# mLSTM gate rows during the retention gate tiles, one scan for samples and prompt, and unread products ahead of TensorE's first operands

## The chip, the cores and the metric

The kernel runs on one core of a Trainium2 chip. The metric is the device time of one execution in microseconds; three executions of the kernel before took 1385.29, 1387.02 and 1387.32 us, median 1387.02. A profiled execution of the same kernel is the source of every row shown. Engines are named as in the profile: PE (TensorE), DVE (VectorE), ACT (ScalarE), POOL (GpSimd), SP (which issues most DMAs here). Each engine works through its own list of instructions in order.

## What is computed

One decoder layer for a prompt of 1024 tokens and for 8 samples of 8 tokens each (1088 token columns in all), width 1024. A combined projection feeds four retention heads and four mLSTM heads of 128; their outputs go through an output projection and a ConvFFN. The part that matters here:

```python
h = rmsnorm(x, pre_mix_g)
proj = (h @ w_in).astype(f32)
q_r, k_r, v_r, g_r, q_m, k_m, v_m, o_m = ...
gates = take(2 * N_ML_HEADS) + b_g.astype(f32)
i_pre, f_pre = gates[..., :N_ML_HEADS], gates[..., N_ML_HEADS:]
...
ret_y = head_groupnorm(ret_out, ret_g) * jax.nn.silu(g_r)
...
logf = jax.nn.log_sigmoid(fg)
def step(carry, inp):
    C, n, m = carry
    qc, kc, vc, ic, lfc = inp
    b = jnp.cumsum(lfc, axis=-1)
    logw = b[..., :, None] - b[..., None, :] + ic[..., None, :]
    logw = jnp.where(causal, logw, -jnp.inf)
    m_t = jnp.maximum(b + m[..., None], jnp.max(logw, axis=-1))
    ...
```

The stabiliser m_t follows the recurrence m_t = max(logf_t + m_(t-1), i_t). For the prompt it starts at -1e30, for each sample at that sample's own m0.

## The kernel before

The kernel is written against a tile framework that derives semaphores from the data and schedules each engine's list from its own time estimates; `issue_after` adds an ordering edge. So the order of the source and the order of an engine's list are not the same.

Tokens are taken in four blocks of 272 columns. A `dense` product (L156 to L160) of one 128-row output tile and one block is 24 matmuls of 128x272: eight slices of the contraction, for each of three terms (high part of the weight by high part of x, low by high, high by low). `proj` loads a weight tile (SP), splits it (high part on ACT, L144; low part on DVE, L146), and runs the four blocks into banks of a pool of two, `psA`; each block is evacuated by a function of its own, and a block's product cannot start before the block two earlier has been read out of its bank.

Opening: pieces of x and the first two weight tiles come in by DMA. For every block, `gain_split` writes the high part of x times a gain (`hh`, ACT, L198) and the low part (`hl`, DVE, L199), and `square_sum` squares x on ACT in two halves (L203) and adds up on DVE for the RMS norm. TensorE starts with the value products of retention heads 0 and 1 (weight tiles `in8` and `in9`), of block 0 in the order of `terms`, evacuated by ACT (`v_r`, L438). `in8_2` is the third block of tile `in8`.

Then follow q and k of retention head 0 (`evac_rot`, ACT L451 and L452, DVE L453 to L455, with rotation and norm), and the gate tiles of the four retention heads, `in12` to `in15`: `early_gate` makes z from the bank on DVE (L469), sigmoid on ACT (L470) and their product y on DVE (L471) for each of 16 tile blocks. Then `gate_proj` projects all mLSTM gates (L316), reads them out (ACT L319, DVE L320 to L322) and adds biases (ACT L323, L324) into two tiles of 4 partitions by 1088: `fg` and `ig`. During it the attention of retention head 0 runs.

`gate_rows` is a generator that turns these rows into what the mLSTM heads need: log sigmoid of the forget gate (ACT L345, L346, L352, L354; DVE L348 to L360), the cumulated sum b per chunk (DVE scan, L368), the stabiliser m by one scan over the prompt (L374) and eight scans of 8 columns over the samples (L378), then differences, exponentials and column copies (L381 to L414). A piece of it is issued at each `next(rows)`, which stands inside the heads that follow. All the while POOL sums up-projection weights in pieces of DRAM and SBUF traffic (`weight_sums`, L715).

Of the kernel before, what the change touches and what calls it, by code (L numbers as in the profile page):

```python
# [16 lines left out]
P = 128  # L17
# [75 lines left out]
def hybrid_layer_kernel(ctx: ExitStack, tc: tile.TileContext, a: dict, o: dict):  # L93
# [4 lines left out]
    def log_exp_tables(after=None):  # L98

        with tc.issue_after(after.ins) if after else nullcontext():  # L100
            nc.scalar.preload_act_table_set("natural_log_exp_and_others")

# [48 lines left out]

    def dense(ps, w, x, b, term=None):

        hi, lo = w
        for k in range(KT):
            ws = slice(k * P, (k + 1) * P)  # L156
            xh, xl = (t[:, k % 4, qcols(b)] for t in x[b // 2][k // 4])
            for i, (u, v) in enumerate(((hi, xh), (lo, xh), (hi, xl))):
                if term in (None, i):
                    nc.tensor.matmul(ps, u[:, ws], v, start=k == i == 0, stop=k == KT - 1 and i == 2)  # L160

    def rstd_small(out, v, w, name, shape):

        l = w.tile(shape, F32, tag="rs_l", name=f"l_{name}")
        nc.scalar.activation(l, v, AF.Ln)
# [27 lines left out]
    def gain_split(x, gain, ops, b):  # L193

        for k in range(KT):
            g = vec[:, gain + k:gain + k + 1]
            hi, lo = (t[:, k % 4, qcols(b)] for t in ops[k // 4])
            nc.scalar.activation(hi, x[:, k, :], AF.Copy, scale=g)  # L198
            nc.vector.scalar_tensor_tensor(lo, x[:, k, :], g, hi.bitcast(F32), ALU.mult, ALU.subtract)  # L199

    def square_sum(x, acc, sq, end=nc.vector):
        for i in range(2):
            nc.scalar.activation(sq[i], x[:, 4 * i:4 * i + 4, :], AF.Square)  # L203
        s, t = sq
# [22 lines left out]
    def tok(name, rows=P, dt=F32):  # L227
        return tokp.tile([P, T], dt, tag="tok", name=name)[:rows, :]


# [26 lines left out]
    sqs = [tok(f"sq{i}").rearrange("p (k n) -> p k n", k=4) for i in range(2)]  # L257
    for b in range(4):
        n = BLK[b][1]
        if b % 2 == 0:  # L260
            h.append(quadrants("h", b // 2))
        gain_split(xs[b], V_PREMIX, h[b // 2], b)
        nts.append(sums[b // 3][:, b % 3 * Q:(b % 3 + 1) * Q])
# [30 lines left out]
    def gate_proj():  # L294
        xst = m2.tile([P, X_SEL], F32, tag="vx", bufs=1, name="xst")
        nc.sync.dma_start(xst, a["cx"][:, :X_SEL])
        xsel = m2.tile([P, X_N - X_SEL], F32, tag="sb", bufs=1, name="xsel")
        nc.sync.dma_start(xsel, a["cx"][:, X_SEL:])
        nc.vector.tensor_copy(idb, ident)
        nc.vector.tensor_copy(negb, xst[:, X_NEG:X_NEG + P])  # L300
        for t in vts:
            nc.gpsimd.memset(t[:, :, P:P + 1], 1.0)
        nc.vector.tensor_copy(negsb, xst[:, X_NEGS:X_NEGS + TS])
        nc.scalar.activation(sel, xsel[:100, :].rearrange("p (j h c) -> p j h c", j=2, h=NH), AF.Copy)
        fg = tok("fg", NH)
        ig = yT[3][:NH, 0, :]
# [17 lines left out]
        nc.scalar.activation(ig, ig, AF.Identity, bias=vec[0:NH, V_BG + 1:V_BG + 2])  # L324

    uihl = mp.tile([100, T], F32R, name="uihl")
    cols = mp.tile([P, 9, 3 * NH], F32, name="cols")
# [12 lines left out]
    def gate_rows():  # L340
        fg, ig = gates
        stk = yT[2][:68, 0, :]
        nc.gpsimd.memset(stk, 0.0)
        e = stk[0:NH, :]
        nc.scalar.activation(e, fg, AF.Abs)  # L345
        nc.scalar.activation(e, e, AF.Exp, scale=-1.0)  # L346
# [6 lines left out]
        rw = yT[3][:NH, 1, :]  # L353
        nc.scalar.activation(rw, w1, AF.Exp, scale=-1.0)  # L354
        nc.vector.tensor_tensor(e, e, rw, ALU.mult)
# [12 lines left out]
        nc.vector.tensor_tensor_scan(bb, rst, lf, 0.0, ALU.mult, ALU.add)  # L368
# [5 lines left out]
        nc.vector.tensor_tensor_scan(mm[:, :LP], lf[:, :LP], ig[:, :LP], NEG, ALU.add, ALU.max)  # L374
        yield
        for s in range(NB):
            sl = slice(LP + s * LS, LP + (s + 1) * LS)
            nc.vector.tensor_tensor_scan(mm[:, sl], lf[:, sl], ig[:, sl], mst[:, 8 + s:9 + s], ALU.add, ALU.max)  # L378
        nc.scalar.activation(stk[0:NH, :], mm, AF.Exp, scale=-1.0)
# [3 lines left out]
        yield  # L383
        nc.sync.dma_start(o["m"], mend)
        u = mm
        nc.vector.tensor_tensor(u, bb, mm, ALU.subtract)
        yield
        aa = bb
        nc.vector.tensor_tensor(aa, ig, bb, ALU.subtract)
        yield  # L390
# [8 lines left out]
        nc.scalar.activation(stk[32:32 + NH, :], aa, AF.Exp)  # L399
        nc.scalar.activation(u, u, AF.Exp)  # L400
        put_rows(1, u)
# [62 lines left out]
    def early_gate(hid):  # L464
        def f(b, ps):
# [3 lines left out]
            nc.vector.tensor_tensor(z, ps, rb[:, o0:o0 + n], ALU.mult)  # L469
            last["sigmoid"] = nc.scalar.activation(y, z, AF.Sigmoid)  # L470
            nc.vector.tensor_tensor(y, y, z, ALU.mult)  # L471
# [19 lines left out]
    def mix_head(hd, ml):  # L491
# [15 lines left out]
        else:  # L507
# [236 lines left out]
    wsums = weight_sums()  # L744
    rows = iter(())
# [620 lines left out]
```

## Time and profile before

| what | us |
|---|---|
| median of three executions | 1387.02 |
| the profiled execution | 1385.24 |
| its span (first to last instruction) | 1383.5 |
| ACT busy | 594.7 |
| POOL busy | 452.4 |

The profiled execution is 1.74 us longer than its span. "Waits" rows read: engine and line that waited, the instruction waited for, then the sum, the count and the longest. Chain rows give start, length and what ran, following back from the last instruction of a window to what released it. Timeline rows give start, length, engine, line, operation, output and inputs, and in brackets the idle time before it with what ended it. A window's row gives the busy time and granted clock of that stretch.

The stages in time, by the profile: first products from 4.78 us, q and k of head 0 behind the values of heads 0 and 1, gate tiles to about 116 us, gates and the attention of head 0 to about 133 us, then retention heads 1 to 3 with the row work.

### The profile page before, as it was taken

How to read it: one execution, taken by the hardware profiler on the slowest of the kernel's cores; microseconds unless marked ns; L12 is line 12 of the kernel's file. 1: busy time of each engine (PE TensorE's matmuls, PEld its weight loads, DVE VectorE, ACT ScalarE, POOL GpSimd, SP SyncE). 2: the span in 40 equal slices, each digit the busy share in tenths (PEclk: the TensorE clock that was granted, in tenths of full speed). 3: DMA queues.
4: the chain of work that ended last, by engine and by line, in shares of the span. 5: the costliest groups of instructions: out<-in, count | busy, mean ns of one | idle time of the engine just before them, and what ended most of it. 6: DMA issues, size and time to landing. Idle time of an engine off the chain costs nothing.

```text
span 1383.5 us, 26841 instructions
## 1 busy us (share of the span) xinstructions
PE 1346.4 (97%) x10545; PEld 1320.3 (95%) x10545; DVE 1010.9 (73%) x2013; ACT 594.7 (43%) x1107; POOL 452.4 (33%) x572
## 2 busy tenths in 40 slices
PE   7999899999999999899999999999999999999995
PEld 7999889999999999899999999999999999999995
DVE  7747986475474366477899988787787788996677
ACT  7524543312322235445465434344344355554563
POOL 1544540379676000000453322222222206872000
PEclk9999999999999999999999999999999999999998
DMA  6444342376986210433214444434444459533363
GB/s 240 138 138 145 119 138 64 110 215 214 199 170 202 62 49 31 159 97 94 98 58 161 148 149 140 131 118 129 151 135 134 132 162 318 185 110 91 97 213 129
DMA packets 93166, 192.80 MB, mean 139 GB/s; under 512 B 16240, under 2 KB 41456, under 8 KB 92528
## 3 DMA queue, kind: packets, MB, share of 16 engines
q1 hardware_dynamic: 80736, 149.03, 33.1%
q0 software_dynamic: 12160, 41.95, 10.7%
q8 instruction: 83, 1.36, 0.4%
q14 instruction: 43, 0.35, 0.1%
q10 hardware_dynamic: 144, 0.11, 0.0%
HBM read 134.58 MB, written 56.47 MB: 138 GB/s over the span
## 4 chain that ended last, share of the span: by engine, by line
PE 88%; DVE 6%; ACT 3%; DMA 1%; issue 1%; SPq 0%; DVEq 0%; ACTq 0%
PE in L160 26%; PE up_S L994 6%; PE up_S L993 6%; PE up_S L992 6%; PE out L160 5%; PE dn L1191 5%; PE dn L1189 5%; PE dn L1190 5%; PE up_A L993 4%; PE up_A L992 4%; PE up_A L994 4%; ACT hh L198 1%; PE up_A L1037 1%; PE up_A L1038 1%; PE up_A L1036 1%
## 5 line engine op out<-in xcount | busy, mean ns | idle before, releaser
L160 PE MATMUL in<-hh,wh_in 128*128 128x272 f32 x1024 | 302.7, 298 | 12.5 <-ACT hh L198 7.9
L160 PE MATMUL in<-hl,wh_in 128*128 128x272 f32 x1024 | 297.0, 293 | 0.0
L160 PE MATMUL in<-hh,wl_in 128*128 128x272 f32 x1024 | 296.9, 292 | 0.0
L160 PEld LDWEIGHTS in<-hh,wh_in 128*128 128x128 f32 x1024 | 194.2, 190 | 17.9 <-ACT hh L198 8.5
L160 PEld LDWEIGHTS in<-hh,wl_in 128*128 128x128 f32 x1024 | 193.8, 190 | 3.6 <-issue 3.5
L160 PEld LDWEIGHTS in<-hl,wh_in 128*128 128x128 f32 x1024 | 193.3, 190 | 1.0 <-issue 0.9
L144 ACT ACTIVATE wh_up<-st_up 128x1024 fp32r<-128x1024 f32 x84 | 80.5, 959 | 162.2 <-PE up_S L993 99.2
L146 DVE TENSOR_TENSOR wl_up<-st_up,wh_up 128x1024 fp32r<-128x1024 f32 x84 | 95.7, 1139 | 9.1 <-ACT wh_up L144 9.1
L966 DVE TENSOR_TENSOR Uv<-Uv,up_S 128x272 f32<-128x272 f32 (+1 forms) x200 | 66.6, 376 | 46.3 <-PE up_S L994 46.3
L1118 DVE TENSOR_TENSOR rb<-rb 128x544 fp32r<-128x544 f32 x78 | 73.7, 950 | 35.1 <-ACT rb L1117 34.9
L1022 POOL TENSOR_TENSOR act<-act 128x544 f32<-128x544 f32 x44 | 70.2, 1595 | 77.5 <-DMA bd<-act 52.6
L715 POOL TENSOR_TENSOR tab<-tab 128x256 f32<-128x256 f32 x104 | 82.6, 805 | 13.0 <-DMA tab<-in_wu 8.4
L1138 POOL TENSOR_TENSOR wd<-wd 128x512 f32<-128x512 f32 x44 | 74.0, 1709 | 26.4 <-issue 11.1
L1117 ACT ACTIVATE rb<-rb 128x544 fp32r<-128x544 f32 x78 | 50.5, 650 | 74.2 <-DMA rb<-bd 67.6
L1007 DVE SCALAR_TENSOR_TENSOR c<-Uv,vec,c 128x1024 f32<-128x1024 f32 (+1 forms) x88 | 70.1, 799 | 8.9 <-ACT c L1005 8.9
L957 POOL MEMSET Ug<- 128x2 f32 x22 | 2.2, 99 | 227.3 <-DVE yT L484 110.8
L715 POOL TENSOR_TENSOR wq<-wq 128x256 f32<-128x256 f32 x56 | 55.4, 999 | 42.3 <-DMA wq<-in_wu 40.0
L1007 DVE SCALAR_TENSOR_TENSOR c<-Ug,vec,c 128x1024 f32<-128x1024 f32 x88 | 67.6, 807 | 1.4 <-ACT c L1005 1.4
L715 POOL DMA_DIRECT2D tab<-in_wu x52 | 36.8, 713 | 77.0 <-DVE k_r L453 57.7
L1005 ACT ACTIVATE c<-Ug,vec 128x1024 f32<-128x1024 f32 (+1 forms) x44 | 34.7, 835 | 52.8 <-DVE Ug L970 47.0
L146 DVE TENSOR_TENSOR wl_in<-st_in,wh_in 128x1024 fp32r<-128x1024 f32 (+2 forms) x33 | 41.5, 1259 | 15.1 <-ACT wh_in L144 15.0
L994 PE MATMUL up_S<-T1h,wl_up 128*128 128x272 f32 x160 | 46.6, 291 | 0.0
(543 smaller groups left out, 4654.5 us busy)
## 6 DMA issues: line engine op xcount, KB each, us to landing
rb<-bd SPq DMA_DIRECT2D x76, 272.0 KB, 2.9
st_up<-sd SPq DMA_DIRECT2D x40, 512.0 KB, 3.9
bd<-act SPq DMA_DIRECT2D x33, 544.0 KB, 4.7
st_in<-in_wi SPq DMA_DIRECT2D x31, 512.0 KB, 4.3
tab<-in_wu POOLq DMA_DIRECT2D x52, 256.0 KB, 4.9
sd<-tab POOLq DMA_DIRECT2D x26, 512.0 KB, 3.6
st_up<-in_wu SPq DMA_DIRECT2D x24, 512.0 KB, 3.5
wd<-in_wd SPq DMA_DIRECT2D x44, 256.0 KB, 4.8
```

What stands on the lines that cost most here:

```text
L144: nc.scalar.activation(hi, x, AF.Copy)
L146: eng.tensor_tensor(lo, x, hi.bitcast(F32), ALU.subtract)
L160: nc.tensor.matmul(ps, u[:, ws], v, start=k == i == 0, stop=k == KT - 1 and i == 2)
L715: last["sums"] = f(*args)
L992: nc.tensor.matmul(ps, wh[:, c], xh[:, k, n], start=k == 0, stop=False)
L993: nc.tensor.matmul(ps, wh[:, c], xl[:, k, n], start=False, stop=False)
L994: nc.tensor.matmul(ps, wl[:, c], xh[:, k, n], start=False, stop=k == 3)
L1007: nc.vector.scalar_tensor_tensor(c, u(i), cw(i), c, ALU.mult, ALU.add)
L1022: nc.gpsimd.tensor_tensor(o_, x, y, ALU.subtract)
L1118: nc.vector.tensor_tensor(lo, x, hi.bitcast(F32), ALU.subtract)
L1138: nc.gpsimd.tensor_tensor(quad(p, out), quad(p, x), quad(p, y), op)
L1189: nc.tensor.matmul(t, wh[:, ms], ah, start=k == 0, stop=False)
```

## The change

- `idle(n)` issues n products of the ones matrix with itself into a bank of its own that nobody reads: 20 before anything else, and 3 after each of the eight slices of the first term of the first product (24 in all). The memset of the ones moves from POOL to DVE.
- The squares of block b are written after the split of block b + 1, and may not be issued before it.
- `gate_proj` moves ahead of the gate tiles, and the pieces of `gate_rows` follow: five at once, one after each gate tile, one behind, the rest in head 0. `fg` lies in a free part of `yT[3]`. The constants that it also loaded go into `gate_consts`, behind head 0.
- The nine scans for m become one over 1088 columns. For that the first column of each sample gets max(ig, lf + m0) as input and -1e30 as its decay, so that the running value before it drops out.
- Sigmoids of the gate tiles are ordered behind the rows' first exponentials, the last exponentials behind the load of the log/exp table.

```diff
+    def idle(n):
+        for _ in range(n):
+            nc.tensor.matmul(warm, ones, ones, start=True, stop=True)
...
-    def dense(ps, w, x, b, term=None):
+    def dense(ps, w, x, b, term=None, wait=0):
...
+            idle(wait)
...
-    nc.gpsimd.memset(ones, 1.0)
+    nc.vector.memset(ones, 1.0)
...
+    warm = bank(psB, P, "warm")
+    idle(20)
...
-    for b in range(4):
+    for b in range(5):
...
-        last["sums"] = square_sum(xs[b], nts[b], sqs, nc.gpsimd if b == 3 else nc.vector)
+            continue
+        nts.append(sums[(b - 1) // 3][:, (b - 1) % 3 * Q:((b - 1) % 3 + 1) * Q])
+        last["sums"] = square_sum(xs[b - 1], nts[-1], sqs, nc.gpsimd if b == 4 else nc.vector)
...
+        aa = rst
+        nc.vector.tensor_tensor(aa, ig, bb, ALU.subtract)
+        yield
         nc.vector.memset(mst[:, 0:1], NEG)
+        heads_of = lambda r: chunked(r)[1][:, :, 0]
+        nc.vector.tensor_tensor(small[:, 3, :8], heads_of(lf), mst[:, 8:16], ALU.add)
+        nc.vector.tensor_tensor(heads_of(ig), heads_of(ig), small[:, 3, :8], ALU.max)
+        nc.vector.memset(heads_of(lf), NEG)
+        mm = rw
+        nc.vector.tensor_tensor_scan(mm, lf, ig, NEG, ALU.add, ALU.max)
         yield
-        nc.sync.dma_start(mst[:, 8:16], a["m0"])
-        mm = rw
-        nc.vector.tensor_tensor_scan(mm[:, :LP], lf[:, :LP], ig[:, :LP], NEG, ALU.add, ALU.max)
-        yield
-        for s in range(NB):
-            sl = slice(LP + s * LS, LP + (s + 1) * LS)
-            nc.vector.tensor_tensor_scan(mm[:, sl], lf[:, sl], ig[:, sl], mst[:, 8 + s:9 + s], ALU.add, ALU.max)
...
                 for i, term in terms or ():
-                    dense(pss[i], ws[i], h, b, term)
+                    dense(pss[i], ws[i], h, b, term, 3 if i == term == 0 else 0)
...
             if hd == 0:
+                gate_proj()
+                for _ in range(5):
+                    next(rows)
                 for i in range(NH):
                     proj((12 + i, early_gate(i)))
+                    next(rows)
                     next(wsums)
                 log_exp_tables(last["sigmoid"])
+                next(rows)
...
         if hd == 0:
-            gate_proj()
-            rows = gate_rows()
+            gate_consts()
```

What it does to the lists. In the rows that follow, a name's number is that of the buffer; `x2` means two such instructions in a row; lines of after are those of the changed file, some 7 to 20 higher.

The opening on ACT, before: `hh` is the high part of x (first digit: pair of blocks), `sq` the squares, `wh_in9` the second weight, `v_r` the evacuation of the value products.

```order
L198 ACTIVATE hh_00_134<-x0_90,vec_66 128x272 x2
L203 ACTIVATE sq0_132<-x0_90 128x1088
L198 ACTIVATE hh_01_136<-x0_90,vec_66 128x272 x4
L203 ACTIVATE sq1_133<-x0_90 128x1088
L144 ACTIVATE wh_in9_124<-st_in9_97 128x1024
L198 ACTIVATE hh_00_134<-x1_91,vec_66 128x272 x4
L198 ACTIVATE hh_01_136<-x1_91,vec_66 128x272 x4
L203 ACTIVATE sq1_133<-x1_91 128x1088
L438 ACTIVATE v_r0_242<-in8_0_244 128x272
```

The same place now:

```order
L205 ACTIVATE hh_00_155<-x0_111,vec_66 128x272 x2
L205 ACTIVATE hh_01_157<-x0_111,vec_66 128x272 x4
L144 ACTIVATE wh_in9_145<-st_in9_118 128x1024
L205 ACTIVATE hh_00_155<-x1_112,vec_66 128x272 x4
L205 ACTIVATE hh_01_157<-x1_112,vec_66 128x272 x4
L211 ACTIVATE sq0_153<-x0_111 128x1088
L211 ACTIVATE sq1_154<-x0_111 128x1088
L205 ACTIVATE hh_10_198<-x2_113,vec_66 128x272 x2
L453 ACTIVATE v_r0_263<-in8_0_265 128x272
```

The squares of x0 moved from between its pieces to behind the split of x1, and the split of x2 begins ahead of the first evacuation. Up to the evacuation of `in8_1` the list held 28 splits and 5 squares before; it holds 30 and 4 now.

DVE at the first gate tile (`in12`), before: z is made from the bank, y from z.

```order
L469 TENSOR_TENSOR z_00_801<-in12_0_776,rb_83 128x272
L471 TENSOR_TENSOR yT0_766<-yT0_766,z_00_801 128x272
L469 TENSOR_TENSOR z_01_830<-in12_1_805,rb_83 128x272
L471 TENSOR_TENSOR yT0_766<-yT0_766,z_01_830 128x272
L469 TENSOR_TENSOR z_02_859<-in12_2_834,rb_83 128x272
```

The same place now, from the second block's z to the fourth's; the operations of 4x1088 are the gate rows, L701 is the state of retention head 0.

```order
L484 TENSOR_TENSOR z_01_981<-in12_1_956,rb_83 128x272
L363 TENSOR_SCALAR yT2_813<-yT2_813 4x1088
L701 SCALAR_TENSOR_TENSOR S_r02_1543<-S_r01_1505,u_r02_1537 128x128
L365 SCALAR_TENSOR_TENSOR yT2_813<-yT2_813 4x1088
L701 SCALAR_TENSOR_TENSOR S_r03_1547<-S_r02_1543,u_r02_1537 128x128
L370 TENSOR_TENSOR yT2_813<-yT2_813,yT3_814 4x1088
L487 TENSOR_TENSOR yT0_811<-yT0_811,z_00_952 128x272
L487 TENSOR_TENSOR yT0_811<-yT0_811,z_01_981 128x272
L372 TENSOR_TENSOR yT2_813<-yT2_813 4x1088
L484 TENSOR_TENSOR z_02_1010<-in12_2_985,rb_83 128x272
L484 TENSOR_TENSOR z_03_1039<-in12_3_1014,rb_83 128x272
```

Four row operations and both earlier y's stand between the second z and the third; L370 and the y's come behind activations of ACT. L363, L365, L370 and L372 of the changed file are L348, L350, L355 and L357 of the one before.

More of the change, by code (lines that the diff above doesn't have):

```diff
@@ L100, in log_exp_tables @@
         with tc.issue_after(after.ins) if after else nullcontext():
-            nc.scalar.preload_act_table_set("natural_log_exp_and_others")
+            last["tables"] = nc.scalar.preload_act_table_set("natural_log_exp_and_others")
     last = {}
@@ L160, in dense @@
                     nc.tensor.matmul(ps, u[:, ws], v, start=k == i == 0, stop=k == KT - 1 and i == 2)
+            idle(wait)
     def rstd_small(out, v, w, name, shape):
         l = w.tile(shape, F32, tag="rs_l", name=f"l_{name}")
-        nc.scalar.activation(l, v, AF.Ln)
+        with tc.issue_after(last["tables"].ins):
+            nc.scalar.activation(l, v, AF.Ln)
         r = w.tile(shape, F32, tag="rs_r", name=f"r_{name}")
@@ L197, in gain_split @@
             hi, lo = (t[:, k % 4, qcols(b)] for t in ops[k // 4])
-            nc.scalar.activation(hi, x[:, k, :], AF.Copy, scale=g)
+            last["hi"] = nc.scalar.activation(hi, x[:, k, :], AF.Copy, scale=g)
             nc.vector.scalar_tensor_tensor(lo, x[:, k, :], g, hi.bitcast(F32), ALU.mult, ALU.subtract)
@@ L202, in square_sum @@
         for i in range(2):
-            nc.scalar.activation(sq[i], x[:, 4 * i:4 * i + 4, :], AF.Square)
+            with tc.issue_after(last["hi"].ins):
+                nc.scalar.activation(sq[i], x[:, 4 * i:4 * i + 4, :], AF.Square)
         s, t = sq
@@ L257, in hybrid_layer_kernel @@
     sqs = [tok(f"sq{i}").rearrange("p (k n) -> p k n", k=4) for i in range(2)]
-    for b in range(4):
-        n = BLK[b][1]
-        if b % 2 == 0:
+    for b in range(5):
+        if b % 2 == 0 and b < 4:
             h.append(quadrants("h", b // 2))
-        gain_split(xs[b], V_PREMIX, h[b // 2], b)
-        nts.append(sums[b // 3][:, b % 3 * Q:(b % 3 + 1) * Q])
+        if b < 4:
+            gain_split(xs[b], V_PREMIX, h[b // 2], b)
         if b == 0:
             split_to(staged[1], *wv[1])
-        last["sums"] = square_sum(xs[b], nts[b], sqs, nc.gpsimd if b == 3 else nc.vector)
+            continue
+        nts.append(sums[(b - 1) // 3][:, (b - 1) % 3 * Q:((b - 1) % 3 + 1) * Q])
+        last["sums"] = square_sum(xs[b - 1], nts[-1], sqs, nc.gpsimd if b == 4 else nc.vector)
     rcol = mp.tile([P, 9], F32, name="rcol")
@@ L294, in gate_proj @@
     def gate_proj():
[L295 to L305, printed above, removed]
+        fg = yT[3][32:32 + NH, 0, :]
         ig = yT[3][:NH, 0, :]
@@ L324, in gate_proj, with gate_consts @@
         nc.scalar.activation(ig, ig, AF.Identity, bias=vec[0:NH, V_BG + 1:V_BG + 2])
+    def gate_consts():
+        xst = m2.tile([P, X_SEL], F32, tag="vx", bufs=1, name="xst")
+        nc.sync.dma_start(xst, a["cx"][:, :X_SEL])
+        xsel = m2.tile([P, X_N - X_SEL], F32, tag="sb", bufs=1, name="xsel")
+        nc.sync.dma_start(xsel, a["cx"][:, X_SEL:])
+        nc.vector.tensor_copy(idb, ident)
+        nc.vector.tensor_copy(negb, xst[:, X_NEG:X_NEG + P])
+        for t in vts:
+            nc.gpsimd.memset(t[:, :, P:P + 1], 1.0)
+        nc.vector.tensor_copy(negsb, xst[:, X_NEGS:X_NEGS + TS])
+        nc.scalar.activation(sel, xsel[:100, :].rearrange("p (j h c) -> p j h c", j=2, h=NH), AF.Copy)
     uihl = mp.tile([100, T], F32R, name="uihl")
@@ L344, in gate_rows @@
         e = stk[0:NH, :]
+        nc.sync.dma_start(mst[:, 8:16], a["m0"])
         nc.scalar.activation(e, fg, AF.Abs)
@@ L353, in gate_rows @@
         rw = yT[3][:NH, 1, :]
-        nc.scalar.activation(rw, w1, AF.Exp, scale=-1.0)
+        last["rows"] = nc.scalar.activation(rw, w1, AF.Exp, scale=-1.0)
         nc.vector.tensor_tensor(e, e, rw, ALU.mult)
@@ L382, in gate_rows @@
         nc.vector.tensor_copy(mst[:, 1:8], mend[:, 0:7])
-        yield
         nc.sync.dma_start(o["m"], mend)
-        u = mm
+        u = bb
         nc.vector.tensor_tensor(u, bb, mm, ALU.subtract)
-        yield
-        aa = bb
-        nc.vector.tensor_tensor(aa, ig, bb, ALU.subtract)
         yield
@@ L398, in gate_rows @@
                 nc.vector.tensor_tensor(v, v, col[:, i0:i0 + 8].unsqueeze(2).broadcast_to([NH, 8, v.shape[2]]), ALU.add)
-        nc.scalar.activation(stk[32:32 + NH, :], aa, AF.Exp)
-        nc.scalar.activation(u, u, AF.Exp)
+        yield
+        with tc.issue_after(last["tables"].ins):
+            nc.scalar.activation(stk[32:32 + NH, :], aa, AF.Exp)
+            nc.scalar.activation(stk[0:NH, :], mm, AF.Exp, scale=-1.0)
+            nc.scalar.activation(u, u, AF.Exp)
         put_rows(1, u)
@@ L469, in f @@
             nc.vector.tensor_tensor(z, ps, rb[:, o0:o0 + n], ALU.mult)
-            last["sigmoid"] = nc.scalar.activation(y, z, AF.Sigmoid)
+            with tc.issue_after(last["rows"].ins):
+                last["sigmoid"] = nc.scalar.activation(y, z, AF.Sigmoid)
             nc.vector.tensor_tensor(y, y, z, ALU.mult)
@@ L744, in hybrid_layer_kernel @@
     wsums = weight_sums()
-    rows = iter(())
+    rows = gate_rows()
     for hd in range(NH):
```

1 line of the change is left out of this document (removed).

## The prediction

> **What bounds the kernel now.** I read the page's busy times first, then PE's waits up to 205 us, then the chain of waits in the two places where PE waits, and last the windows and the timelines there. In the windows the columns are the window, its length, busy time (x instructions) of PE, PEld, DVE, ACT and POOL, then granted clock, DMA share and GB/s.
>
> ```profile
> PE 1346.4 (97%) x10545; PEld 1320.3 (95%) x10545; DVE 1010.9 (73%) x2013; ACT 594.7 (43%) x1107; POOL 452.4 (33%) x572
> ...
> PE in L160 <- ACT hh L198: 7.9, 3, 4.8
> PE in L160 <- DVE k_r L453: 3.8, 2, 2.7
> PE in L160 <- ACT v_r L438: 0.7, 1, 0.7
> PE x_r L538 <- DVE k_r L455: 0.4, 1, 0.4
> ...
> 0.00:25.20 25.20, 16.57 (x96) 15.10 (x96) 18.12 (x38) 21.14 (x41) 2.00 (x11) 1.00 0.90 329
> 68.70:115.70 47.00, 47.00 (x378) 47.00 (x377) 19.94 (x38) 10.44 (x21) 21.60 (x27) 1.00 0.40 135
> 161.70:166.40 4.70, 4.69 (x25) 4.69 (x26) 4.70 (x15) 1.79 (x3) 1.81 (x3) 0.64 0.32 112
> ```
>
> The kernel is bound by TensorE: 1346.4 us busy of 1383.5. In the part that the change touches PE waits only twice: for its first operands (7.9 us on the split of x, 0.7 on an evacuation) and in head 1 for DVE (3.8 + 0.4). Between 68.7 and 115.7, the retention gate tiles, PE is never idle and DVE is busy for 19.94 of 47 us. So the change can win only in the opening and in head 1, and can lose in the gate tiles.
>
> In the opening the chain (start, length, what) runs through ACT, not PE:
>
> ```profile
> 2.61 4.90 DMA x<-in_x
> ...
> 7.53 0.94 ACT hh L198 x2
> 8.47 1.00 ACT sq L203
> 9.47 1.65 ACT hh L198 x4
> 11.12 1.00 ACT sq L203
> 12.12 0.95 ACT wh_in L144
> ...
> 24.89 0.29 ACT v_r L438
> ...
> 25.22 12.45 PE in L160 x97
> ```
>
> The piece of x landed at 7.51; from 7.53 ACT works without a pause until 25.18, when it has evacuated the second block of the first value product; that frees the bank for which PE waits. From 25.22 PE runs through.
>
> PE's pace there, by its timeline (start, length of the group, x matmuls):
>
> ```profile
> 11.56 2.02 PE L160 MATMUL in<-hh,wl_in 128*128 128x272 f32 x8
> 13.37 2.02 PE L160 MATMUL in<-hl,wh_in 128*128 128x272 f32 x8
> ...
> 16.34 1.15 PE L160 MATMUL in<-hh,wl_in 128*128 128x272 f32 x8
> 17.33 1.15 PE L160 MATMUL in<-hl,wh_in 128*128 128x272 f32 x8
> ```
>
> Eight products start in 1.81 us at first (0.227 each) and in 0.99 us later (0.124): half pace, then full.
>
> In head 1 the chain is DVE's:
>
> ```profile
> 156.13 2.20 DVE yT L374
> 158.33 2.98 DVE yT L378 x7
> 161.31 0.35 DVE k_r L453
> ...
> 161.71 4.81 PE in L160 x24
> ```
>
> The prompt's scan and seven sample scans stand on DVE ahead of the k_r that frees PE's bank. Behind the wait the clock is 0.64 for 4.70 us (third window), which costs 4.70 x 0.36 = 1.7 us. The stage thus loses 3.8 + 0.4 + 1.7 = **5.9 us**.
>
> **The change part by part.** The sum is made against the profiled execution, 1385.24 us (span 1383.5 and 1.74 around it); the median of the runs, 1387.02, lies 1.78 above it, and I carry differences over to the median.
>
> *Opening, squares a block later.* ACT needs 1.65 us for four hh, 0.41 each, and 1.00 for a square. Up to the decisive evacuation the order has 28 hh and 5 squares before, 30 hh and 4 squares after: 2 x 0.41 - 1.00 = -0.2. But the squares at 8.47 and 11.12 filled time in which ACT would have waited for x and for the second weight tile:
>
> ```profile
> st_in<-in_wi SPq DMA_DIRECT2D x1, 512.0 KB, 6.6
> ```
>
> Issued at 4.04, it lands at 10.6; without the square ACT is there at 10.3, a wait of 0.3; and about 0.2 more goes to the next piece of x0, which I estimate at 8.7, 1.2 behind the one at 7.51. -0.2 + 0.5 = **+0.3**. Bounds: -0.7 if both waits vanish and another 0.5 of slack in the chain turns up, +1.5 if the later pieces of x are each late too.
>
> *Opening, unread products.* A plain f32 128x128 product is two matmul records:
>
> ```profile
> 119.65 0.39 PE L672 MATMUL o_r<-vts,pt_r 128*128 128x128 f32 x2
> 119.87 0.39 PE L667 MATMUL u_r<-vts,kz_r 128*128 128x128 f32 x2
> ```
>
> That is 0.22 us each at full pace, 0.44 at half. 20 + 8 x 3 = 44 of them are 9.7 us; PE idles for 25.20 - 16.57 = 8.6 and would save 24 x 0.10 = 2.4 of half pace, so they about fit. PE's walk: from 1.2 (an estimate, just behind the memset of the ones), some ten at 0.44 and ten at 0.22, to 7.8; the first term 8 x (0.125 + 0.66) = 6.3, to 14.1; 40 products at 0.125, to 19.1; two more tiles of 24, to 25.1. ACT's walk by the order ends at 25.5. So PE arrives warm and waits: the products cost nothing while ACT's chain covers them, and gain nothing for the same reason. Without that cover each costs 0.22, the last 24 together 5.3.
>
> *Gate rows.* Gates are projected ahead of the gate tiles, and the row operations stand between their z's on the in-order DVE. Their durations, from both stages:
>
> ```profile
> 74.84 0.44 DVE L469 TENSOR_TENSOR z<-in,rb 128x272 f32<-128x272 f32 x1 [1.65 <-PE in L160]
> 77.84 0.44 DVE L469 TENSOR_TENSOR z<-in,rb 128x272 f32<-128x272 f32 x1 [1.62 <-PE in L160]
> 80.25 0.97 DVE L471 TENSOR_TENSOR yT<-yT,z 128x272 f32<-128x272 f32 x1
> ...
> 115.53 1.28 ACT L101 ACT_TABLE_LOAD   x1
> 134.99 1.21 ACT L323 ACTIVATE fg<-fg,vec 4x1088 f32<-4x1088 f32 x1 [0.18 <-DVE fg L321]
> ...
> 141.50 0.72 DVE L348 TENSOR_SCALAR yT<-yT 4x1088 f32<-4x1088 f32 x1
> 142.69 1.61 DVE L350 SCALAR_TENSOR_TENSOR yT<-yT 4x1088 f32<-4x1088 f32 x1
> 147.81 1.27 DVE L355 TENSOR_TENSOR yT<-yT,yT 4x1088 f32<-4x1088 f32 x1
> ...
> 162.95 2.40 DVE L368 TENSOR_TENSOR_SCAN yT<-yT,fg 4x1088 f32<-4x1088 f32 x1
> ...
> 173.57 1.85 DVE L389 TENSOR_TENSOR yT<-yT,yT 4x1088 f32<-4x1088 f32 x1
> ```
>
> PE makes a tile block in 3.0 us (74.84 to 77.84) and has two banks, so the first block of the second gate tile waits for the third z of the first. Ahead of that z stand, in order, L348, L350, two row activations on ACT, L355, two y's and L357. From the end of the gate products: ACT has 2.1 us of other work (a weight's high part, 0.95 as in the chain, and three evacuations of about 0.4), then four row activations of about 1.1, to 6.5; two blocks of PE (6.0) with some 1.0 of head-0 products and the second z, to 7.5; L348, a state update and L350, to 9.7; Ln and Exp, to 11.9; L355, to 13.2, and meanwhile a table load (1.28) and two sigmoids for the y's, to 14.5; L357, to 15.8; z, to 16.2. PE has four blocks and nine plain products, 12.1 + 2.0 = 14.1, so it waits **2.2** (the z ends at 16.2); half pace behind it, as behind the 2.7 us wait, costs 1.7. From there to the seventh next z DVE has two scans (4.8), six row operations at 1.27 (7.6), a row memset (1.0), fourteen z's and y's (6.2), two weight splits, taken like row operations (2.5), and some fifteen small ones (2): 24.1 us, against seven blocks' 21.2, or 22.9 with the slow clock: **1.2** more. After loses 5.1, before lost 5.9: **-0.8**. Bounds: no loss at all (-5.9), or the longer durations throughout (L471 0.97, L389 1.85): stall 4.1, clock 1.7, tail 4, so 9.8 and +3.9. I take the walk, since its rows are of the very operations.
>
> The waiting DVE instruction holds the z's behind it, and PE waits for those. In head 1 the rows are gone from DVE, so no k_r is late; what is next late there is another bank; I price it at nothing, and at most at the smaller of the two waits of before, 3.8 - 2.7 = 1.1.
>
> [...]
>
> *One scan for samples and prompt.* 2.20 + 2.98 on DVE become one scan of 1088 (2.40, as L368's) and four operations on 4x8, which I put at 0.1 each (at most 0.43, as the small scans): 2.4 us less, which the 24.1 holds already. *The rest at nothing:* the constants' two DMAs, copies and activation move behind head 0 and are read first by the mLSTM heads, so the rest of the retention heads covers them; the memset of the ones lies on a DVE that has no x yet; POOL's zeroing of the row tiles stands at its queue's start in both orders; the m0 load and the m store are one issue each on SP. The m store waits for the rows' ends on DVE and holds the weight load of the next k tile behind it, which has the rest of the gate tiles as cover; without it the load would be late by a row operation or two, 1.3 to 2.6 us.
>
> Sum: +0.3 - 0.8 = -0.5, 1384.7 by the profiled execution and **1386.5** on the median.
>
> **The rivals.** (1) *The rows all fit*: DVE is busy for only 42% of the gate tiles, and if the table load and activations overlap better than in my walk no z is late. -5.9 + 0.3 gives 1381.4. Against it: the first stall comes from a chain through ACT, not from DVE's load. (2) *Slower: the rows hold the z's.* The in-order DVE passes POOL's delays on to the bank: 9.8 instead of 5.9, with the opening +4.2, 1391.2. It decides from a first stall of about 4 us on, when the rows run as L389 did. (3) *PE's clock sets the opening*, and the unread products buy the 2.4 us of half pace: -2.4 - 0.8, 1383.8.
>
> ```profile
> 665.95 0.72 PE L185 MATMUL ssqb_po<-oacc,ones 128*128 128x272 f32 x2 [1.79 <-DVE oacc L831]
> ...
> 667.76 0.43 PE L1036 MATMUL up_A<-B1h,wh_up 128*128 128x272 f32 x1
> 667.99 0.43 PE L1037 MATMUL up_A<-B1l,wh_up 128*128 128x272 f32 x1
> ```
>
> Here a gap of 1.79 us was followed by half pace (0.23 apart), so pauses matter; but the chain up to 25.22 is ACT's, which speaks against it. [...] (4) *The change doesn't do what it says*: the unread products do not lift the clock. PE then has 20 x 0.44, 8 x (0.23 + 1.32), 16 x 0.227, 24 x 0.125 and 6.0: from 1.2 to 35, +9.8, 1396.
>
> **How the numbers follow.** 0.2%, 2.8 us, is about what a measurement of this kernel can tell from no change. Chances: forecast 0.50 (its own range 1384.2 to 1389.8), rows fit 0.22, clock 0.10, rows hold 0.14, unread products cold 0.04. Faster is rows fit and clock, 0.32; same 0.50; slower 0.18. The range reaches 0.8 past the first rival and the second, 1380.6 to 1392.0, and leaves out the fourth (0.04) and about two fifths of those two at their own spread (0.14), under 0.2 in all.
>
> **What would show it.** Opening: products at 0.125 from the first term on, and PE waiting for v_r near 25.5; a start of that tile before 23 would prove the clock right. Gate tiles: a PE wait of about 2 us for the third z, a clock near 0.6 behind it, DVE busy for over 80%. Head 1: no wait for k_r. The prediction is wrong if PE has no wait in the gate tiles, if waits of over 4 us stand there, or if the opening ends before 23 or after 28.

## The result, and the profile after

The changed kernel took 1391.93 us, median of 12 runs (1386.34 to 1395.05), against 1386.53 (1383.88 to 1387.85) for the kernel before in the same rounds: ratio 1.0039, 95% interval [1.0026, 1.0052], slower by 5.4 us. The profiled execution took 1391.41, 6.2 above the 1385.24 of before; its span is 1389.6.

In what follows, places are compared by the start of the same PE product in both profiles, counted along PE's list without the unread products (10,545 in each). Before, the third block of the first value tile (`in8_2`, the place where the prediction's opening ends) starts at 25.22.

The page of after, busy time by engine:

```profile
PE 1355.2 (98%) x10633; PEld 1329.6 (96%) x10633; DVE 1006.3 (72%) x2009; ACT 596.1 (43%) x1107; POOL 445.6 (32%) x571
```

PE's records rose by 88: the 44 unread products, two records each. PE's waits in after up to 205 us:

```profile
PE in L165 <- DVE z L484: 4.0, 3, 1.9
PE warm L155 <- DVE ones L182: 1.1, 1, 1.1
PE in L165 <- DVE q_r L468: 0.5, 1, 0.5
PE in L165 <- ACT v_r L453: 0.5, 1, 0.5
PE in L165 <- DVE k_r L468: 0.2, 1, 0.2
```

The 7.9 us of waits for the split of x are gone, and 0.2 is left of the k_r waits of head 1; waits for z have come in.

The opening of after, on PE's timeline:

```profile
1.06 7.05 PE L155 MATMUL warm<-ones 128*128 128x128 f32 x40 [1.06 <-DVE ones L182]
...
14.24 1.25 PE L165 MATMUL in<-hh,wl_in 128*128 128x272 f32 x8
15.33 1.16 PE L165 MATMUL in<-hh,wh_in 128*128 128x272 f32 x8
...
26.21 0.39 PE L165 MATMUL in<-hh,wh_in 128*128 128x272 f32 x1 [0.47 <-ACT v_r L453]
```

The unread products fill PE from 1.06 on, and behind the first term eight products start in about 1.1 us instead of 1.81: PE is close to the full pace of the prediction's rows (0.99), as it said. And it waits for v_r, as the prediction said, but until 26.21: 1.0 later than before.

The gate tiles of after, on PE's timeline:

```profile
93.45 0.36 PE L165 MATMUL in<-hh,wh_in 128*128 128x272 f32 x1 [1.92 <-DVE z L484]
...
94.85 0.43 PE L165 MATMUL in<-hh,wl_in 128*128 128x272 f32 x1
95.08 0.43 PE L165 MATMUL in<-hl,wh_in 128*128 128x272 f32 x1
```

and the window over them (columns as in the prediction):

```profile
68.70:115.70 47.00, 42.96 (x330) 42.09 (x328) 40.03 (x76) 20.30 (x32) 24.86 (x24) 0.96 0.34 113
```

The first wait is 1.92 us, products start 0.23 apart behind it (half pace), and DVE is busy for 40.03 of 47 us, 85%.

All this answers to steps of the prediction, and none of it makes 5.4 us. Counted along PE, after is late by 1.0 at `in8_2`, 0.8 at 230 us, 2.2 at 404, 1.8 at 690, and then loses 4.5 us at one place: between products 8800 and 8900, at about 1150 us, in the down projection of the ConvFFN, which the change does not touch. There the waits of PE in after have two rows that before lacks:

```profile
PE dn L1210 <- DVE rb L1138: 1.6, 1, 1.6
PE dn L1211 <- DVE ra_dlo L1138: 1.3, 1, 1.3
```

On PE's timeline of after:

```profile
1158.32 0.39 PE L1210 MATMUL dn<-rb,ra_dlo 128*128 128x272 f32 x1 [1.62 <-DVE rb L1138]
...
1160.00 0.59 PE L1211 MATMUL dn<-rb,ra_dlo 128*128 128x272 f32 x1 [1.29 <-DVE ra_dlo L1138]
...
1160.62 0.43 PE L1210 MATMUL dn<-rb,ra_dlo 128*128 128x272 f32 x1
1160.85 0.43 PE L1211 MATMUL dn<-rb,ra_dlo 128*128 128x272 f32 x1
```

Two waits, 2.9 us, and half pace behind them: from 1159.65 on the granted clock is 0.50 for 3.4 us, which costs 1.7. 2.9 + 1.7 = 4.6, against the 4.5 lost. One step back, DVE there in after:

```profile
1146.47 0.69 DVE L1138 TENSOR_TENSOR ra_whi<-wd,ra_whi 128x512 fp32r<-128x512 f32 x1 [0.84 <-ACT ra_whi L1137]
1147.08 2.38 DVE L1034 TENSOR_TENSOR act<-c 128x1088 f32<-128x1088 f32 x1
1149.39 1.81 DVE L1138 TENSOR_TENSOR rb<-rb 128x544 fp32r<-128x544 f32 x1
```

and before:

```profile
1144.41 1.28 DVE L1014 TENSOR_TENSOR act<-c 128x1088 f32<-128x1088 f32 x1
1145.61 0.72 DVE L1118 TENSOR_TENSOR rb<-rb 128x544 fp32r<-128x544 f32 x1
```

POOL's sums of the down projection's weights in after:

```profile
1146.57 1.75 POOL L1158 TENSOR_TENSOR wd<-wd 128x512 f32<-128x512 f32 x1 [12.07 <-issue]
```

and before, two of them in one row:

```profile
1143.91 5.27 POOL L1138 TENSOR_TENSOR wd<-wd 128x512 f32<-128x512 f32 x2 [11.13 <-issue]
```

DVE waits 0.84 us for ACT's `ra_whi`, and then `act` and the `rb` behind it take 1.1 us more each. 0.84 + 1.1 + 1.1 = 3.0, against 2.9 of waits on PE. POOL's sum and `act` overlap in both kernels, but the one that takes longer has changed: before, POOL's two sums take 5.27 and `act` keeps 1.28; after, POOL's first takes 1.75 and `act` 2.38. Of the 22 `act`s of each kernel this is the only one beside a sum of POOL, and 2.38 is the only one of the 44 that is not 1.28 or 1.29. What makes the one or the other take longer is not shown. Another step back, ACT's waits between 1136 and 1160 us in after:

```profile
ACT ra_whi L1137 <- DMA wd<-in_wd: 1.9, 1, 1.9
ACT ra_wlo L1137 <- DMA wd<-in_wd: 1.9, 1, 1.9
```

Before, the first of them isn't there:

```profile
ACT ra_wlo L1117 <- DMA wd<-in_wd: 1.3, 1, 1.3
ACT ra_dlo L1117 <- DMA wd<-in_wd: 0.8, 1, 0.8
```

So a piece of the down projection's weight (`wd`) came late: ACT began to read it 5.1 us behind its issue, 3.2 before. ACT, DVE and POOL shifted against each other, and PE waited. Which part of the change reaches 1140 us? From the output projection to 1360 us the lists of the engines are the same but for one place near 575 us, where a weight split of ACT, a sum of DVE and 25 products of PE stand in another order. What else differs is in the DMA queues. The page of after, section on queues:

```profile
q8 instruction: 84, 1.38, 0.4%
```

and that of before:

```profile
q8 instruction: 83, 1.36, 0.4%
```

On this queue 83 packets of 16 KB came in before, for 21,090 weight loads and matmuls of PE (10,545 of each), and 84 after, for 21,266: one in about 254. I take them for loads of PE's own instructions, one for each 256; before_tiny64, below, with 256 instructions more, agrees: its load stands 2.6 us ahead of the weight load's issue, where before has it. 44 unread products are 88 weight loads and 88 matmuls, 176 instructions, so every later load comes 176/256 of a period (16 us before, from 1136.25 to 1152.30), some 11 us, earlier in PE's work.

The DMA queues in the 5 us from the issue of that weight load, in after:

```profile
q1 hardware_dynamic: 649, 1.23, 80.7%
q8 instruction: 1, 0.02, 1.7%
```

and before:

```profile
q1 hardware_dynamic: 641, 1.21, 78.2%
```

After, an instruction load begins 2.2 us behind the issue; before, it had begun 2.6 us ahead of it. That is the **loads theory**: the unread products move the loads of PE's instructions, one of them meets the weight load and makes it late. The rivals: the gate rows hold z's (the prediction's own second rival), the opening is late by order alone, and the order near 575 us makes the place slow.

### The profile page after: what moved, and what is told of

Its sections match the earlier page's. It is cut to its first block, busy times and chain, and to the rows that moved or that the text cites. A ratio compares the mean times of both kernels' runs of the same rounds, so it can differ in the third digit from the quotient of the medians.

```text
span 1389.6 us, 27023 instructions
## 1 busy us (share of the span) xinstructions
PE 1355.2 (98%) x10633; PEld 1329.6 (96%) x10633; DVE 1006.3 (72%) x2009; ACT 596.1 (43%) x1107; POOL 445.6 (32%) x571
## 4 chain that ended last, share of the span: by engine, by line
PE 86%; DVE 7%; ACT 3%; DMA 2%; issue 2%; SPq 0%; DVEq 0%; ACTq 0%
PE in L165 25%; PE up_S L1014 6%; PE up_S L1013 6%; PE up_S L1012 6%; PE out L165 5%; PE dn L1211 5%; PE dn L1209 5%; PE dn L1210 4%; PE up_A L1013 4%; PE up_A L1012 4%; PE up_A L1014 4%; DMA x<-in_x 1%; PE up_A L1057 1%; PE up_A L1058 1%; PE up_A L1056 1%
## 5 line engine op out<-in xcount | busy, mean ns | idle before, releaser
L146 DVE TENSOR_TENSOR wl_up<-st_up,wh_up 128x1024 fp32r<-128x1024 f32 x84 | 94.7, 1127 | 9.6 <-ACT wh_up L144 9.6
L736 POOL TENSOR_TENSOR tab<-tab 128x256 f32<-128x256 f32 x104 | 79.4, 774 | 14.3 <-DMA tab<-in_wu 9.8
```

The lines of the kernel that those rows point to most:

```text
L146: eng.tensor_tensor(lo, x, hi.bitcast(F32), ALU.subtract)
L736: last["sums"] = f(*args)
```

## The experiments

Every kernel computes all the outputs. "Third slice" is the place between products 8800 and 8900. Ratios are to the kernel before, with 95% intervals. The expectations name their theories by letters: A, the time is lost where the change was made; B, it is lost in the down projection, which shifts against POOL's work; B', the later opening by itself does that; C, the loads theory; D, the unread products make the scheduler put more splits ahead of ACT's evacuation.

### Repeats, and the two halves

`before_again` and `after_again` are the two kernels unchanged.

> The kernel before, unchanged, for a second profile and the scatter of its runs. Theory A (the time is lost where the change was made: opening, gate tiles, mLSTM heads): ratio 1.000, and the waits of the down projection on the low parts made by DVE (2.9 us and 1.7 us of half clock in the profile of after) may be here too. Theory B (the time is lost in the down projection, which the change shifts against POOL's work): ratio 1.000 and no such wait here, as in the first profile of before.

> The changed kernel, unchanged, for a second profile. Theory A: ratio 1.002 to 1.005, opening again 1.0 us later than before, gate tiles again with waits of about 4 us for z; the wait in the down projection need not come back. Theory B: the wait of 2.9 us in the down projection and the half clock behind it come back.

`open_only` is the kernel before with the opening's part of the change, the later squares included:

```diff
-    nc.gpsimd.memset(ones, 1.0)
+    nc.vector.memset(ones, 1.0)
...
+    warm = bank(psB, P, "warm")
+    idle(20)
...
-    for b in range(4):
+    for b in range(5):
...
-                    dense(pss[i], ws[i], h, b, term)
+                    dense(pss[i], ws[i], h, b, term, 3 if i == term == 0 else 0)
```

> The kernel before with only the opening of the change: 44 unread products, the ones set by DVE, squares a block later. Theory A: the third value block starts 1.0 us later, ratio 1.0007. Theory B: the same shift at the start, and the waits in the down projection appear, ratio 1.003 to 1.005.

`rows_only` is the changed kernel with these lines put back.

> The changed kernel with the opening of before: no unread products, the ones set by POOL, squares in their old place; gates, rows and the one scan stay as changed. Theory A: at the start of head 2 between -0.5 and 0 us against before, then the 1.4 us that after lost by 404 us in the mLSTM heads, ratio 1.001. Theory B: ratio as after (1.003 to 1.005) if the shift by the rows sets it, 1.000 if the opening does.

Measured: before_again 1.0001 [0.9987, 1.0014], after_again 1.0029 [1.0016, 1.0043], open_only 1.0026 [1.0013, 1.0038], rows_only 1.0005 [0.9994, 1.0016]. The loss is at the place of theory B, and nearly all of it comes from the opening's part of the change. PE's waits of open_only between 1140 and 1165 us:

```profile
PE dn L1202 <- DVE ra_dlo L1129: 1.3, 1, 1.3
PE dn L1201 <- DVE rb L1129: 1.2, 1, 1.2
```

It loses 0.8 us at `in8_2` and 5.4 in the third slice; rows_only loses nothing at either place, though it has all of the row work. That the rows hold the z's is true of both kernels with early rows, but it is not where the 5.4 us went.

### The opening taken apart

`squares_only` is the kernel before with only the squares a block later; `fill_only` only with the unread products and their ones; `no_fill` is the changed kernel without the unread products:

```diff
-    warm = bank(psB, P, "warm")
-    idle(20)
...
-                    dense(pss[i], ws[i], h, b, term, 3 if i == term == 0 else 0)
+                    dense(pss[i], ws[i], h, b, term)
```

> The kernel before with the squares a block later and no unread product. Theory C: no wait in the down projection; the third value block starts 0.3 to 1.0 us later than before, ratio 1.0002 to 1.0007. Theory B': the later opening brings the waits, ratio 1.002 to 1.004.

> The kernel before with the 44 unread products alone (the ones set by DVE, squares in their old place). Theory C: waits of 2 to 3 us in the down projection with slow clock behind. Theory D: the list of ACT has 30 splits and 5 squares ahead of the evacuation of in8_1 (28 and 5 before), so the third value block starts about 0.8 us later. Ratio 1.002 to 1.004. If the products paid by the clock: third value block up to 2.4 us earlier.

> The changed kernel without its 44 unread products; squares a block later, early rows and the one scan stay. Theory C: no wait in the down projection; theory D (the unread products make the scheduler put six splits and a square of ACT ahead of the evacuation of in8_1): the third value block starts 1 to 2 us earlier than before instead of 1.0 us later. Together ratio 0.998 to 1.000, against 1.003 to 1.004 for the changed kernel. If the unread products do shorten the opening: slower than the changed kernel by up to 2.4 us.

Measured: squares_only 0.9982 [0.9972, 0.9992], fill_only 1.0023 [1.0012, 1.0033], no_fill 1.0011 [0.9999, 1.0023]. At `in8_2` they stand at -1.8, +1.0 and -2.0 us; in the third slice at 0, +1.9 and 0. ACT's evacuation of `in8_1`, which frees the bank for `in8_2`, on ACT's timeline of squares_only:

```profile
22.22 0.37 ACT L440 ACTIVATE v_r<-in 128x272 f32<-128x272 f32 x1
```

and of after:

```profile
25.78 0.38 ACT L453 ACTIVATE v_r<-in 128x272 f32<-128x272 f32 x1
```

For squares_only an opening 0.3 to 1.0 later was expected: a miss. Late squares alone win the opening; with unread products the win turns into a loss. ACT's order tells why: ahead of that evacuation stand 24 splits and 3 squares in squares_only and no_fill, 30 and 4 in after, 30 and 5 in fill_only. The scheduler, with products ahead of PE's work, put six more splits and a square first, 6 x 0.41 + 1.00 = 3.5 us by the prediction's own durations; 25.78 - 22.22 = 3.56 was measured.

no_fill's opening came as expected, its total did not: it lies 0.0029 above squares_only, about 4 us, and the early rows are nearly all that parts the two (in its profile 2.9 us lost between 52 and 404 us, where squares_only gains 1.2). rows_only, with the same rows, puts them at 0.7 us. The size of the rows' cost stays open between these; a gain is seen in neither.

### Moving the instruction loads alone

`before_tiny44` is the kernel before with 44 unread products so small that they take PE 4.7 us of the time in which it has no operands, 176 instructions; `before_tiny64` has 64, which makes 256, a whole load. `after64` fills the changed kernel's unread products up to 64:

```diff
+    def tiny(n):
+        for _ in range(n):
+            nc.tensor.matmul(warm[:32, :32], ones[:, :32], ones[:, :32], start=True, stop=True)
...
-    nc.gpsimd.memset(ones, 1.0)
+    nc.vector.memset(ones, 1.0)
...
+    warm = bank(psB, P, "warm")
+    tiny(44)
```

In after64, `idle(20)` is `idle(14)` and `tiny(26)`.

> The kernel before with 44 unread products of 32x32 ahead of the first operands (the ones set by DVE), where PE waits anyway; nothing else changes, and the opening should end as before (25.2 us). They are 176 instructions of PE, as many as those of the change. Theory C (the loads of PE's instructions, one of 16 KB every 256 instructions, move in time and meet a weight load of the down projection): such a load at 1140 to 1143 us, the waits of 2.5 us and slow clock in the down projection, ratio 1.002 to 1.004. Theory B' (the later opening shifts the rest): no such wait, ratio 1.000.

> The same with 64 such products, 256 instructions, one whole block. Theory C: the loads of instructions fall where they fell in the kernel before (near 1136 and 1152 us), no wait in the down projection, ratio 1.000. If any 44 or more unread products cost the time by themselves: as with 44, or more.

> The changed kernel with 14 unread products of 128x128 and 26 of 32x32 in place of the first 20, so 64 in all and 256 instructions, with about the same time of PE ahead of x. Theory C: loads of instructions near 1136 to 1138 us, no wait in the down projection, ratio 1.000 to 1.0015 (the opening's 1.0 us less what the rows give). Theory B': as after, 1.003 to 1.004.

Measured: before_tiny44 1.0015 [1.0004, 1.0025], before_tiny64 0.9999 [0.9991, 1.0008], after64 1.0019 [1.0010, 1.0027]. At `in8_2` the first two lose 1.2 and 0.2 us, in the third slice 3.8 and nothing. PE's waits of before_tiny44 between 1140 and 1165 us:

```profile
PE dn L1199 <- DVE ra_dlo L1126: 1.3, 1, 1.3
PE dn L1198 <- DVE rb L1126: 0.8, 1, 0.8
```

before_tiny64 has no such row, and no load of instructions in the 5 us behind the weight load's issue. The medians of the two, 1388.92 and 1386.63 in the same rounds, differ by 2.3 us; 1.0015 is less than the 1.002 to 1.004 expected. That before_tiny44 loses 1.2 us at `in8_2`, where nothing was expected, isn't explained.

after64 has no such row either. Its 1.0019 lies above the range expected: it is late by 2.8 us already at `in8_2`, behind 32 splits and 4 squares on ACT, out of 4.8 at the end of its profile. Though its opening ends 1.8 us later than that of after, its median ratio is 0.0010 to 0.0020 lower than the two measured for the changed kernel (1.0029 and 1.0039).

### 20 products, and the best parts together

`before_tiny20` has `tiny(20)`, 80 instructions. `squares_scan` is squares_only with the change's row code, the one scan included, left at its old place in heads 1 to 3.

> The kernel before with 20 unread products of 32x32 ahead of x, 80 instructions of PE. Theory C: loads of instructions 5 us earlier than before, near 1131 and 1147 us; neither meets the weight load at 1138 to 1143, so no wait of over 1 us in the down projection and ratio 0.999 to 1.001. If the number of unread products alone counts, between none (1.000) and 44 (1.0015).

> The kernel before with the squares a block later and with the gate rows of the changed kernel (one scan, the difference taken ahead of it) in their old place, in heads 1 to 3; no unread products. As squares alone in the opening (1 us earlier); on DVE in head 1 some 2.4 us of scans less, so the waits for k_r shrink from 3.8 to 1 to 2 us. Ratio 0.996 to 0.999; if k_r is held by the other rows, as squares alone, 0.998.

Measured: before_tiny20 1.0018 [1.0007, 1.0028], squares_scan 0.9980 [0.9971, 0.9989], 1382.88 us. squares_scan beats both kernels. What the one scan adds is not shown by the medians, since squares_only has 0.9982 without it; its waits for k_r fell to 2.9 us, not to the 1 to 2 expected, and its profile ends 1.5 us ahead of that of squares_only. before_tiny20 is a miss: it has no wait in the third slice and nothing lost at `in8_2`, and yet it is slower. Its waits up to 205 us show

```profile
PE in L165 <- DVE k_r L461: 3.5, 1, 3.5
PE in L165 <- DVE q_r L461: 1.3, 1, 1.3
PE yt_r L624 <- DVE on_r L622: 0.9, 1, 0.9
PE x_r L546 <- DVE k_r L463: 0.7, 1, 0.7
```

where before has 3.8 for k_r and 0.4 for x_r alone. Counted along PE it is on time at 140 us and 2.4 us late at 180, about what its ratio says (2.5). So its loss stands in head 1, with DVE; why 20 products bring it about isn't settled.

### New kernels for the loads theory

Four kernels with 176 unread instructions had the wait, in five profiled executions, and those without any, with 80 or with 256 had none. Four more tested it: `tiny(108)` is 432 instructions, 256 + 176; `tiny(52)` is 208 and `tiny(36)` 144; `scan_tiny44` is squares_scan with `tiny(44)`.

> 108 unread products of 32x32 ahead of the first operands: 432 instructions, 256 and 176, so the loads of PE's instructions should stand where 44 such products put them, 1.7 to 2.4 us behind the issue of the weight load of the down projection's third slice. Loads theory: that slice shows PE waits for rb and ra_dlo of 2 to 3 us in sum and loses 2 to 6 us against before; the products themselves take about 10.5 us by the 0.049 each of before_tiny64 and may push the opening by 0 to 2, so 1.001 to 1.005. Rival, the loss comes from something else that 44 products do: no waits there (0 to 0.4 us), 1.000 to 1.0015.

> The best kernel (late squares, one scan; 0.998) with 44 unread 32x32 products ahead: 176 instructions. Loads theory: the load 1.7 to 2.4 us behind the weight load's issue, waits for rb and ra_dlo of 2 to 3 us in the third slice of the down projection, a loss there of 2 to 6 us against squares_scan; with an opening that may lose up to 3 as in fill_only, 0.999 to 1.003. Rival: no waits there, only the opening's loss, 0.998 to 1.000.

> 52 products, 208 instructions: the load would stand about 0.4 us behind the weight load's issue. Loads theory: the two start together, so the wait for the weight and PE's waits appear, perhaps smaller, 0.5 to 3 us; 1.0005 to 1.003. Rival: no waits, 0.999 to 1.001.

> 36 products, 144 instructions: the load would stand about 4.4 us behind the weight load's issue, when most of the weight has landed. Loads theory: small or no waits there, 0 to 1.5 us; 0.9995 to 1.002. Rival, the count of unread instructions: waits near those of 44, 2 to 2.5 us.

Measured: before_tiny108 1.0003 [0.9990, 1.0015], scan_tiny44 0.9982 [0.9963, 1.0001], before_tiny52 1.0000 [0.9991, 1.0009], before_tiny36 0.9999 [0.9989, 1.0009]. PE's waits of scan_tiny44 between 1138 and 1168 us:

```profile
PE dn L1201 <- DVE ra_dlo L1128: 1.3, 1, 1.3
PE dn L1200 <- DVE rb L1128: 1.2, 1, 1.2
```

and of before_tiny108:

```profile
PE dn L1199 <- DVE ra_dlo L1126: 1.4, 1, 1.4
PE dn L1198 <- DVE rb L1126: 0.2, 1, 0.2
```

The other two have none. In the profiles the theory holds, with a narrower place than expected: a load that begins 0.2 us behind the weight load's issue does no harm (before_tiny52, for which waits of 0.5 to 3 us were expected), nor one at 5.5 (before_tiny36). The totals of the two with waits lie with the rival: their profiled executions, 1389.85 and 1388.94, stand above their medians of 1385.33 and 1386.84. So each was profiled once more.

> The kernel of scan_tiny44 unchanged, one more profiled execution. If the loss in the down projection's third slice stands in every execution: waits for rb and ra_dlo of 1.5 to 3 us there, a loss of 3 to 5 us against squares_scan, and a time of 1386 to 1390. If it stands in some only: no such wait and a time of 1382 to 1386 is as likely.

> The kernel of before_tiny108 unchanged, one more profiled execution. In every execution: waits for rb and ra_dlo of 1 to 3 us in the third slice and a time of 1387 to 1390. In some only: no such wait and a time of 1382 to 1387 is as likely.

Measured, one execution each: 1391.46 us, over the range expected, and 1388.07, within it, with these waits of PE between 1138 and 1168 us in scan_tiny44_again:

```profile
PE dn L1200 <- DVE rb L1128: 1.5, 1, 1.5
PE dn L1201 <- DVE ra_dlo L1128: 1.3, 1, 1.3
```

and 1.3 and 1.3 in before_tiny108_again. All profiled executions together, by where the load of instructions begins (us from the issue of the weight load) and what the third slice loses:

| profiled executions | unread instructions | load begins | PE's waits | third slice |
|---|---|---|---|---|
| after, after_again, open_only, fill_only, before_tiny44 | 176 | +1.7 to +2.4 | 1.8 to 2.9 | +1.9 to +5.7 |
| scan_tiny44, scan_tiny44_again | 176 | +2.1, +2.2 | 2.5, 2.8 | +4.2, +4.3 |
| before_tiny108, its repeat | 432 | +2.0, +2.3 | 1.6, 2.6 | +3.2, +2.8 |
| before, before_again, and four kernels without unread products | 0 | -2.6 to -2.3 | at most 0.2 | -0.4 to +0.1 |
| before_tiny64, after64 | 256 | -2.6, -2.8 | at most 0.2 | -0.4 to 0.0 |
| before_tiny52 | 208 | +0.2 | none | -0.2 |
| before_tiny36 | 144 | +5.5 | none | -0.1 |
| before_tiny20 | 80 | -8.8, +9.1 | at most 0.2 | -0.4 to 0.0 |

Nine of nine with the load near +2 lose there, none of eleven others does. The steps behind it are the same in all nine: ACT begins to read the weight 4.3 to 5.1 us behind its issue and `act` takes 2.38 to 2.40 us on DVE; in the eleven others these are 3.0 to 4.0 and 1.28 to 1.29. (DVE's wait of 0.84 in after is not in all nine; open_only has none.) PE's waits and half of the time at half clock behind them (none, 3.4 or 6.8 us) make up each loss to within 0.5 us. The order near 575 us doesn't decide: before_tiny108 loses without it, and six kernels that do not lose have it (no_fill, squares_only, squares_scan, before_tiny64, after64, before_tiny52).

What each loses in the median of its timed runs is less uniform: unread products cost 0.0044 on squares_only (which makes it open_only), 0.0018 or 0.0028 on no_fill (which makes it after, by its two measurements) and 0.0023 on before, but between before and before_tiny108, and between squares_scan and scan_tiny44, the ratios differ by less than their intervals. Whether some executions escape the wait was not seen in a profile and stays open. So does how the two loads meet: the traces show that they lie side by side and that the weight is then read later, not what the one does to the other.

## Why the prediction was wrong, point by point

The forecast was 1386.5, no change; it came out 5.4 us slower, at the upper end of the range and on the side to which it gave 0.18.

- **The opening, "+0.3".** The mechanism was right: ACT's chain sets the end, PE arrives close to full pace (eight products in about 1.1 us) and waits for v_r. No row of before shows the walk's ten products at 0.44 and ten at 0.22, an estimate; in after eleven of the 20 took 0.44 each, to 5.9 us, and nine 0.22, to 7.87. The size was +1.0. The squares were worth -1.8 to -2.0 by themselves; the unread products took that back through ACT's order. The prediction counted that order (30 and 4 against 28 and 5) without asking which part of the change made it.
- **"The products cost nothing while ACT's chain covers them."** This is the step that failed. It priced the products as time on PE, of which they indeed cost none. It left out that they are 176 instructions which shift every later load of instructions; in the profile this cost 4.5 us at 1150 us (5.7 in the repeat), most of the 6.2. The waits behind it, the load's place and the doses of 0 to 432 instructions show it for the profiled executions; the medians agree for most of the kernels and not for before_tiny108 and scan_tiny44. The products also cost 3.0 us at `in8_2` by ACT's order (+1.0 in after, -2.0 in no_fill).
- **The gate rows, "-0.8".** The first wait was forecast at 2.2 and is 1.92, with the half pace foreseen; the later waits for z are 2.1 where 1.2 stood, and q_r 0.5 and k_r 0.2 came in. With 1.7 for the clock, after loses 4.0 + 0.5 + 0.2 + 1.7 = 6.4 where before lost 5.9. Counted along PE from 50 to 200 us, which holds both stages, after gains 0.5, its repeat 1.2 and rows_only nothing, while before_again, the kernel before unchanged, gains 0.5 too. So the place and the first size were right, and whether these stages gain the 0.8 isn't shown; rows_only's 1.0005 [0.9994, 1.0016] and no_fill's 1.0011 show no gain in all. In the walk 16.2 - 14.1 is 2.1, not 2.2, and 7.5 + 0.72 + 1.61 is 9.8 without the state update, not 9.7.
- **The rest at nothing.** No wait of PE for the constants, the m0 load or the m store showed. But the five profiles with early rows (after, after_again, rows_only, no_fill, after64) all lose 0.9 us more between 200 and 390 us, in small steps without a wait of PE; what makes it was not traced. "The rest" held the whole program behind the mixer, though, and 4.5 us came out of it.
- **The rivals.** *Rows all fit* fell with the wait of 1.92. *Rows hold the z's* gave 1391.2, within a microsecond of the result, but that is luck: its first stall of 4 us did not come. What it calls POOL's delays stands in the trace of before: of the 16 `y`s of the gate tiles the 12 that no sum of POOL overlaps took 0.44 each, the other four 0.58 to 0.98; the `z`s took 0.43 or 0.44 with and without one. *PE's clock sets the opening* fell: PE was close to full pace and gained nothing, and in squares_only the opening is 1.8 us shorter without any unread product. *Unread products cold* fell with the nine at 0.22.

Sum by the profile: +1.0 opening, +0.8 more up to 690 us, +4.5 in the third slice, -0.2 behind it: +6.1 of 6.2.

## What to carry to other kernels

Here instructions that cost PE no time where they stand moved every later load of its instructions (near 1140 us from 2.6 ahead of a weight load's issue to 2.2 behind it), and this one came to stand beside a weight load that was needed soon. Where transfers are as tight as there (80.7% of the DMA engines' time in those 5 us), compare a run with a whole load's worth of them (256 here) against a run with fewer before you trust either result. And take the parts of a change apart even when the sum is a loss: here the late squares alone make 0.9982, and with one scan, left at its old place, 0.9980, while the parts meant to fill PE took more than that back.

## What the runs showed of the hardware that was not expected

Behind waits of PE the granted clock was 0.50 for 3.4 us, which cost 1.7, three times in each of the two profiles: from 162.3, 568.5 and 667.5 us in before, from 94.7, 688.6 and 1159.65 in after. Behind the waits of the third slice in after_again and open_only it was 6.8 us. Each of the six began 0.6 to 1.5 us behind the end of a gap of 1.62 to 2.66 us; but the same gap is not followed by it alike each time. Before, behind the wait for the first output weight, on PE's timeline:

```profile
567.59 0.39 PE L160 MATMUL out<-mh,woh 128*128 128x272 f32 x1 [2.43 <-ACT woh L144]
```

with the window behind it:

```profile
568.50:571.90 3.40, 3.05 (x13) 3.05 (x14) 1.87 (x3) 0.64 (x1) 0.00 (x0) 0.50 0.53 166
```

After, nearly the same gap on PE's timeline:

```profile
569.61 0.39 PE L165 MATMUL out<-mh,woh 128*128 128x272 f32 x1 [2.29 <-ACT woh L144]
```

with the window behind it:

```profile
570.00:574.00 4.00, 3.13 (x25) 3.14 (x26) 2.39 (x3) 1.16 (x2) 0.00 (x0) 1.00 0.43 135
```

The granted clock is 0.50 in the first and 1.00 in the second. The waits of 1.6 and 1.3 us in the third slice, and that of 1.92 in the gate tiles, were followed by it; before_tiny108_again had waits of 1.3 and 1.3 without it and lost 2.8 there, while before_tiny108, with waits of 1.6 in all and half pace behind them, lost 3.2. Such differences may be part of why single executions of the changed kernel lie up to 8.7 us apart; that was not traced further.
